# A two-layer decoder trunk: gate and up products as seven block products, and bias matmuls of 128 rows

## The chip, the cores and the metric

The kernel runs on one core of one Trainium2 chip. The metric is device time in microseconds of one launch, as the median of several runs; beside it there is one execution taken with the hardware profiler, from which all rows come. The engines are TensorE (PE; its weight loads are listed apart as PEld), VectorE (DVE), ScalarE (ACT), GpSimd (POOL) and SyncE (SP, which here only issues DMAs). A matmul takes a stationary operand of up to 128 x 128 (loaded by an LDWEIGHTS) and streams a moving operand of up to 512 columns through it, into a bank of PSUM (128 x 512 in fp32; eight banks).

## The reference

Two layers on 512 tokens of width 1024, in fp32. Each layer does, cut to what matters:

```python
z = x @ w_in + b_in                        # 11648 columns: q, k, v, gates ...
y_a = dilated window attention (3 groups of 6 heads), combined by softmax denominators
y_b = silu(g_r) * group_norm(retention(q_r, k_r, v_r))     # 4 heads
mix = (sigmoid(gate_a) * (y_a @ w_attn_proj) + sigmoid(gate_b) * (y_b @ w_ret_proj)) @ w_out
x = layer_norm(ALPHA * x + mix)
ffn = (silu(x @ w_gate) * (x @ w_up)) @ w_down             # w_gate, w_up: 1024 x 2816
x = layer_norm(ALPHA * x + ffn)
```

## The kernel before

**Precision.** Each fp32 operand is split into a high part (rounded to the matmul's format, by a ScalarE cast, L92 or L319) and a low part (the rest, by a VectorE subtraction, L93 or L325). A product a·b is three matmuls: high·high, high·low, low·high (`mm3`). x lies transposed in `xh` and `xl` (width in chunks of 128 down the partitions, tokens across), weights come by DMA into `raw` tiles (128 x 1024, eight buffers) and are split into `whi` and `wlo` (four buffers each; `unit`).

**Order.** The tile framework lays down each engine's instruction order when the kernel is built, from its own estimate of durations: among instructions it expects to be ready it takes the one that the program emits first, so a later one can move ahead into a gap. Small work (attention steps, transposes, block sums) is put between matmuls by hand: functions wait in a list `side`, and `tick`, called after every three matmuls, pops them at a set rate (`pace`). `drain` pops the rest. Each engine then runs its queue strictly in that order.

**The two ways to make a product with a weight matrix.** `wstat` makes 128 output columns for all 512 tokens: 8 chunks x 3 matmuls of 512 columns, weights stationary. `wstat_halves` does the same for four outputs in two halves of 256 tokens, for the start of a stage, where the later tokens of x aren't there yet. `tall` makes a 2 x 2 block product by the Strassen-Winograd scheme, with x stationary: seven products instead of eight, over sums S1 to S4 of blocks of x (kept in `xs`, made by `x_sums` from plain copies of x, `xc`) and sums P1 to P4 of blocks of the weights. P1 and P3 are summed by an accumulating DMA that GpSimd issues (L310), P2 and P4 by VectorE (L336). The products run in this order and add up in three PSUM chains, A, X and C:

```python
ORDER = ((1, "A11", "B11"), (2, "A12", "B21"), (5, "S1", "P1"), (3, "S4", "B22"),
         (6, "S2", "P2"), (7, "S3", "P3"), (4, "A22", "P4"))
CHAIN = {1: "A", 6: "A", 7: "A", 4: "A", 2: "X", 5: "C", 3: "C"}
```

The partial results of products 1, 5 and 6 are copied out by ScalarE (L422) before the chain goes on; after product 7 VectorE subtracts (L429). In `tall` each chain is two PSUM tiles, one for each half of the tokens (`a` in 0, 1), and the halves alternate. `tall` is used for the attention's v (288 columns a block) and for the retention's values and gates (512 a block). There, a bias is added by a matmul that opens chains A and C: `ones` (33 x 128, ones in the first and last row) times `bh` (33 rows; the first holds the high part of the bias, the last the low part, the rest zero). There are 48 of these in a launch. `bias_rows` fills them.

**The feed-forward network.** Its 2816 hidden columns are done in three parts of 3, 4 and 4 pairs of 128 (`FPARTS`); a pair needs 256 columns of gate and of up, two outputs each. The first pair goes through `wstat_halves`, the others through four `wstat`. Silu by ScalarE (L1007), the product with up by VectorE (L1012), and a split give `ht`; then the part's down projection (`xstat`) adds into the residual. The first layer norm's result reaches `xh`, `xl` by transposes (`to_xT`), four token tiles one after the other.

**The start, and the attention's tail.** At the start of layer 0, x comes in four token tiles and the first weights in four quarters; `pair_units(..., apart=True)` splits the weights quarter by quarter. In the attention, each pair of heads ends with a tail of seven steps, put between the next pair's steps at given places: `swapped` and `weighed` are DMAs on ScalarE's queue, through DRAM; `weigh` combines the groups' denominators; `scale` and `place` apply them.

Of the kernel before, what the change touches and what calls it, by code (L numbers as in the profile page):

```python
# [18 lines left out]
P = 128  # L19
# [29 lines left out]
BK = 33  # L49
# [4 lines left out]
def hybrid_kernel(ctx, tc, x, rel_bias, w_in, b_in, w_attn_proj, w_ret_proj, w_out,  # L54
# [15 lines left out]
    ones = keep.tile([BK, P], F32R, name="ones")  # L70
    bh = keep.tile([BK, 1024], F32R, name="bh")
# [124 lines left out]
    def pair_units(w, c, c2=None, apart=False):  # L196
# [9 lines left out]
        if c2 is not None:  # L206
            todo = [(hf, q) for hf in range(2) for q in range(2)]
            for hf, q in sorted(todo, key=lambda t: t[::-1]) if apart else todo:
                nc.sync.dma_start(vs[hf][:, :, q * P:(q + 1) * P], w[:, 4 * hf:4 * hf + 4, (c, c2)[q]:(c, c2)[q] + P])
        if not apart:  # L210
            return [unit(v) for v in vs]
        out_ = [tuple(view(wp.tile([P, 1024], F32R, tag=t, name=t), 4, 256) for t in ("whi", "wlo")) for _ in vs]
        for q in range(2):
            for v, (h, l) in zip(vs, out_):
                cs = slice(q * P, (q + 1) * P)
                hilo(v[:, :, cs], h[:, :, cs], l[:, :, cs])
        return out_
# [77 lines left out]
    class Right:  # L295
# [33 lines left out]
        def begin(self, n):  # L329

            if n == "B11":
                self.load("B11", "B21", "P1", "B22", "P3")
            elif n in ("P2", "P4"):
                for u in range(len(self.shapes)):
                    r = self.t["P1", u]
                    dve.tensor_tensor(out=r, in0=r, in1=self.t["B22" if n == "P2" else "B21", u], op=ALU.add)  # L336
            return self.high(n)
# [47 lines left out]

    def run(g):
        for _ in g:
            pass
# [10 lines left out]
    def bias_rows(b1, b2):  # L399

        n = b1.shape[0]
        r = raw("rb")[:BK, :2 * n]
        pool.memset(r, 0.0)
        for q in (0, BK - 1):
            pool.dma_start(r[q:q + 1, :n], b1.unsqueeze(0))
            pool.dma_start(r[q:q + 1, n:], b2.unsqueeze(0))
# [3 lines left out]
        e = slice(BK - 1, BK)  # L410
# [58 lines left out]
    def attention_pair(hp, qk, v, yp, bias, yaT):  # L469
# [107 lines left out]
        tail = [swapped, weigh, weighed, lambda: scale(0), lambda: place(0), lambda: scale(1), lambda: place(1)]  # L577
# [15 lines left out]
    def layer(ly, cp):  # L593
# [65 lines left out]
        with stage("attn") as ap_, stage("attw", 4) as aw:  # L659
# [5 lines left out]
            def qk_units(hp, g, apart=False):  # L665
                c = g * GW + hp * P
                return pair_units(w_l, C_QA + c, C_KA + c, apart)
# [9 lines left out]
            if ly == 0:  # L677
# [18 lines left out]
                us0 = [qk_units(0, 0, True)]  # L696
                load_x(2)
                us0.append(qk_units(0, 1))
                load_x(3)
# [6 lines left out]
                dve.memset(o32[:BK, :P], 0.0)  # L706
                dve.memset(o32[0:1, :P], 1.0)
                dve.memset(o32[BK - 1:BK, :P], 1.0)
                act.copy(out=ones, in_=o32[:BK, :P])
# [55 lines left out]
            for hp in range(HPG // 2):  # L765
# [10 lines left out]
                for at, f in zip((24, 22, 15, 14, 12, 8, 3), reversed(tail)):  # L776
# [5 lines left out]
            side.extend(n * 3 + tail[:1] + n * 4 + tail[1:2] + n * 3 + tail[2:5] + n * 6 + tail[5:6] + n * 2 + tail[6:])  # L782
# [211 lines left out]
        cp = []  # L994
        for part, (f0, f1) in enumerate(FPARTS):
            ht = []
            for fpair in range(f0 // 2, f1 // 2):
                ug, uu = pair_units(wg_l, fpair * 256), pair_units(wu_l, fpair * 256)
                if fpair == 0:
                    pgs = wstat_halves([(u, e) for u in (ug, uu) for e in range(2)])  # L1000
                    ln_par(ln2_g[ly], ln2_b[ly])
                else:
                    pgs = [wstat(ug, e) for e in range(2)]
                ts = []
                for e in range(2):
                    t = work("sl")
                    act.activation(out=t, in_=pgs[e], func=AF.Silu)  # L1007
                    ts.append(t)
                for e in range(2):
                    pu = pgs[2 + e] if fpair == 0 else wstat(uu, e)  # L1010
                    t = ts[e]
                    dve.tensor_tensor(out=t, in0=t, in1=pu, op=ALU.mult)  # L1012
                    o_ = fo.tile([P, 2, S], F32R, tag="op", name="ht")
                    hilo(t, o_[:, 0], o_[:, 1])
                    ht.append(o_)
                drain()

            def h_tok(k, i, ht=ht):
                return ht[k][:, 0, i * P:(i + 1) * P], ht[k][:, 1, i * P:(i + 1) * P]
# [79 lines left out]
```

## Time and profile before

| | before |
|---|---|
| runs | 2248.61 us median of 3 (2247.89 to 2251.42) |
| the profiled execution | 2250.18 us, its span 2248.4 us |
| TensorE busy | 2223.7 us, 10890 matmuls |
| weight loads busy | 1841.0 us |
| VectorE, ScalarE, GpSimd busy | 1184.3, 844.7, 180.8 us |
| DMA | 294.23 MB, 131 GB/s on average |

A row of a timeline gives start, duration, engine, line, operation and "output<-inputs", shapes, and in brackets the idle time before it with what ended it. Rows of groups give count, then total busy time and the mean of one in ns, then idle time before them by what ended it. Matmul ends are modelled, so one row's time overlaps the next; the distance between starts is what a matmul takes in a stream.

### The profile page before, as it was taken

The numbers are of one execution on the slowest core, as the hardware profiler recorded it, in microseconds if no ns is written. First come the engines' busy times: TensorE is split into PE (matmuls) and PEld (weight loads), VectorE is DVE, ScalarE is ACT, GpSimd is POOL, SyncE is SP. The second block draws the span as 40 slices with busy tenths as digits, with TensorE's granted clock in tenths as the row PEclk, the third lists the DMA queues.
The fourth block names the chain that finished last, engine by engine and source line by source line (L and its number), as shares of the span: only waits on it lengthen the run. The fifth ranks groups of instructions, "written<-read, shape, count | busy, mean of one in ns | idle before, by whom it ended". The sixth has DMA issues, their size and how long they took to land.

```text
span 2248.4 us, 27714 instructions
## 1 busy us (share of the span) xinstructions
PE 2223.7 (99%) x10890; PEld 1841.0 (82%) x10890; DVE 1184.3 (53%) x1795; ACT 844.7 (38%) x1373; POOL 180.8 (8%) x240
## 2 busy tenths in 40 slices
PE   8999999999999999999999999999999999999998
PEld 7977778878888888888889777788888888888886
DVE  5643677776245543334376446777743455333345
ACT  4444544545333132223145445445543232222230
POOL 3110011110000100000030100111000001000001
PEclk9999999999999999999999999999999999999999
DMA  7943365555655133333159343565455552333320
GB/s 213 240 128 83 74 161 151 140 133 158 216 178 187 57 113 94 94 95 111 47 155 248 98 91 86 146 167 144 125 172 195 193 169 66 101 89 101 103 76 38
DMA packets 261602, 294.23 MB, mean 131 GB/s; under 512 B 21517, under 2 KB 199841, under 8 KB 261344
## 3 DMA queue, kind: packets, MB, share of 16 engines
q1 hardware_dynamic: 212928, 234.13, 35.0%
q0 software_dynamic: 21264, 45.54, 9.1%
q10 hardware_dynamic: 27280, 12.80, 2.0%
q8 instruction: 85, 1.39, 0.3%
q14 instruction: 45, 0.37, 0.1%
HBM read 266.63 MB, written 28.53 MB: 131 GB/s over the span
## 4 chain that ended last, share of the span: by engine, by line
PE 74%; issue 16%; DMA 4%; DVE 3%; POOL 1%; ACT 1%; POOLq 0%; DVEq 0%; ACTq 0%
PE ps L81 66%; PE px L81 6%; DMA raw<-in_w_in 2%; PE px L502 1%; POOL ry L124 1%; PE px L833 1%; DMA exd<-wb 1%; DMA fa<-exd 1%; DVE wlo L325 1%; DVE xtok L926 1%; DMA rb<-in_b_in 0%; DMA exd<-pk 0%; DMA mb<-exd 0%; DVE stats L937 0%; PE px L169 0%
## 5 line engine op out<-in xcount | busy, mean ns | idle before, releaser
L81 PE MATMUL ps<-xh,whi 128*128 128x512 f32 (+1 forms) x1760 | 674.8, 385 | 7.1 <-ACT xh L92 7.1
L81 PE MATMUL ps<-xh,wlo 128*128 128x512 f32 (+1 forms) x1760 | 659.7, 375 | 1.0 <-DVE wlo L93 1.0
L81 PE MATMUL ps<-xl,whi 128*128 128x512 f32 (+1 forms) x1760 | 659.6, 375 | 0.2 <-DVE xl L93 0.2
L93 DVE TENSOR_TENSOR wlo<-raw,whi 128x1024 fp32r<-128x1024 f32 (+2 forms) x274 | 330.8, 1208 | 528.2 <-ACT whi L92 527.7
L92 ACT CAST whi<-raw 128x1024 fp32r<-128x1024 f32 (+2 forms) x274 | 282.8, 1035 | 462.9 <-PE ps L81 399.6
L81 PEld LDWEIGHTS ps<-xh,whi 128*128 128x128 f32 x1760 | 332.1, 189 | 71.3 <-ACT xh L92 8.3
L81 PEld LDWEIGHTS ps<-xh,wlo 128*128 128x128 f32 x1760 | 332.2, 189 | 61.2 <-DVE wlo L93 1.2
L81 PEld LDWEIGHTS ps<-xl,whi 128*128 128x128 f32 x1760 | 333.1, 189 | 53.7 <-DVE xl L93 1.0
L81 PE MATMUL ps<-whi,xs 128*128 128x512 f32 (+1 forms) x768 | 221.9, 363 | 0.0
L325 DVE TENSOR_TENSOR wlo<-raw,whi 128x1024 fp32r<-128x1024 f32 (+1 forms) x168 | 178.7, 1064 | 81.1 <-ACT whi L319 80.3
L319 ACT CAST whi<-raw 128x1024 fp32r<-128x1024 f32 (+1 forms) x168 | 154.2, 923 | 118.8 <-PE ps L81 92.6
L81 PE MATMUL ps<-whi,ht 128*128 128x512 f32 x576 | 178.3, 389 | 0.0
L81 PEld LDWEIGHTS ps<-whi,xs 128*128 128x128 f32 x768 | 137.7, 188 | 24.1 <-ACT whi L319 2.2
L81 PE MATMUL ps<-wlo,xs 128*128 128x512 f32 (+1 forms) x384 | 138.0, 359 | 0.4 <-DVE wlo L325 0.4
L124 POOL TENSOR_TENSOR ry<-ve,mhalf 128x1 f32<-128x1 f32 x48 | 44.8, 944 | 1152.0 <-DVE ve L123 1152.0
L81 PEld LDWEIGHTS ps<-whi,ht 128*128 128x128 f32 x576 | 108.1, 188 | 22.4
L81 PE MATMUL ps<-wlo,ht 128*128 128x512 f32 x288 | 112.0, 389 | 0.0
L81 PE MATMUL ps<-whi,xh 128*128 128x512 f32 (+1 forms) x288 | 106.7, 370 | 1.9 <-DVE sn L429 1.9
L81 PE MATMUL ps<-wlo,xh 128*128 128x512 f32 (+1 forms) x288 | 103.2, 358 | 0.0
L81 PE MATMUL ps<-whi,xl 128*128 128x512 f32 (+1 forms) x288 | 103.0, 358 | 0.0
L310 POOL DMA_DIRECT2D raw<-in_w_in x48 | 59.2, 1234 | 293.0 <-DMA raw<-in_w_in 204.0
L81 PEld LDWEIGHTS ps<-wlo,xs 128*128 128x128 f32 x384 | 72.2, 188 | 9.6 <-DVE wlo L325 0.9
(167 smaller groups left out, 2518.9 us busy)
## 6 DMA issues: line engine op xcount, KB each, us to landing
raw<-in_w_in SPq DMA_DIRECT2D x144, 512.0 KB, 4.0
raw<-in_w_ffn_gate SPq DMA_DIRECT2D x44, 512.0 KB, 3.8
raw<-in_w_ffn_up SPq DMA_DIRECT2D x44, 512.0 KB, 3.8
raw<-in_w_ffn_down SPq DMA_DIRECT2D x44, 512.0 KB, 3.7
raw<-in_w_in SPq DMA_DIRECT2D x72, 256.0 KB, 5.3
raw<-in_w_in POOLq DMA_DIRECT2D x32, 512.0 KB, 7.4
raw<-in_w_ret_proj SPq DMA_DIRECT2D x32, 512.0 KB, 3.9
raw<-in_w_in SPq DMA_DIRECT2D x40, 288.0 KB, 4.3
```

What stands on the lines that cost most here:

```text
L81: pe.matmul(ps, lhsT=a, rhs=b, start=start, stop=stop, skip_group_check=True)
L92: act.copy(out=hi, in_=src)
L93: dve.tensor_tensor(out=lo, in0=src, in1=hi.bitcast(F32), op=ALU.subtract)
L124: pool.tensor_tensor(out=y, in0=ve, in1=mhalf, op=ALU.pow)
L310: pool.dma_start(r, self.src({"P1": "B12", "P3": "B22"}[n], u), accum_op=ALU.add)
L319: act.copy(out=h, in_=src)
L325: dve.tensor_tensor(out=l, in0=src, in1=h.bitcast(F32), op=ALU.subtract)
L502: pe.transpose(px[:, (2 + j) * P:(3 + j) * P], s[:, hh, j * P:(j + 1) * P], ident)
L833: pe.transpose(px[:, t * P:(t + 1) * P], ys[i][:, t * P:(t + 1) * P], ident)
L926: dve.scalar_tensor_tensor(out=o_, in0=o_, scalar=rs, in1=b_[:, c:c + n], op0=ALU.mult, op1=ALU.add)
```

## The change

Every gate/up pair but a layer's first becomes one seven-product block product (`wide`, `ffn_pair`), with the weights stationary and x's blocks moving: the "1" columns are up and the "2" columns gate, 256 each; the token halves are x's blocks. A chain is one PSUM tile, with the two 128-column halves (`q`) side by side. The x copies `xc` and block sums are now also made after the first layer norm. The bias matmuls get 128 rows, with the low part in row 32 as before. P3 is loaded ahead of B22. At the start of layer 0 two token tiles are transposed before the first weights are split, the bias columns' buffers come from the work pool, and the attention's tail steps move in the list.

```diff
-BK = 33
+BK = 32
-    ones = keep.tile([BK, P], F32R, name="ones")
-    bh = keep.tile([BK, 1024], F32R, name="bh")
+    ones = keep.tile([P, P], F32R, name="ones")
+    bh = keep.tile([P, 1024], F32R, name="bh")
...
-                self.load("B11", "B21", "P1", "B22", "P3")
+                self.load("B11", "B21", "P1", "P3", "B22")
...
+    def wide(right, left, ev):
+
+        ps = {}
+        for (i, an, bn), ((h, l),) in zip(ORDER, right.operands()):
+            c = CHAIN[i]
+            if i in FIRST:
+                ps[c] = psum("ps")
+            for q in range(2):
+                cs = slice(q * P, (q + 1) * P)
+                for k in range(4):
+                    ah, al = left(an, k, slice(0, 256))
+                    mm3(ps[c][:, q * 256:(q + 1) * 256], h[:, k, cs], l[:, k, cs], ah, al,
+                        i in FIRST and q == 0 and k == 0, k == 3)
+                    tick(STEP / 2)
+            if i != 3:
+                ev(i, ps[c])
+            if i == 6:
+                ev(3, ps["C"])
+            yield
...
-        tail = [swapped, weigh, weighed, lambda: scale(0), lambda: place(0), lambda: scale(1), lambda: place(1)]
+        tail = [swapped, weigh, lambda: scale(0), lambda: place(0), weighed, lambda: scale(1), lambda: place(1)]
...
-        braws.append(sm.tile([COLS // P, P], F32, tag="braw", name="braw", bufs=2))
+        braws.append(work("braw")[:COLS // P, :P])
...
-                for f in ops[0]:
+                for f in ops[0] + ops[1]:
                     f()
-                side.extend(ops[1] + [lambda l_=l_: bias_cols(l_) for l_ in range(DEPTH)] + vecs[:3] + ops[2] + vecs[3:] + ops[3])
+                make()
+                us0 = [first, qk_units(0, 1)]
+                load_x(3)
+                side.extend([lambda l_=l_: bias_cols(l_) for l_ in range(DEPTH)] + vecs[:3] + ops[2] + vecs[3:] + ops[3])
...
-                for at, f in zip((24, 22, 15, 14, 12, 8, 3), reversed(tail)):
+                for at, f in zip((26, 24, 18, 16, 14, 12, 3), reversed(tail)):
...
+            xc = [[mp.tile([P, 4, 256], F32, name=f"xc{a}{b}") for b in range(2)] for a in range(2)]
...
-                        side.extend([nothing] * (6, 2, 4, 5)[i] + to_xT(xt[:, i], i, None))
+                        side.extend([nothing] * (6, 2, 4, 5)[i] + to_xT(xt[:, i], i, xc))
...
-        fo = fin.enter_context(stage("fo", 11))
+        fo = fin.enter_context(stage("fo", 5))
...
+        def ffn_plain(f, o_):
+
+            ug, uu = pair_units(wg_l, f * P), pair_units(wu_l, f * P)
+            pgs = wstat_halves([(u, e) for u in (ug, uu) for e in range(2)])
+            drain()
+            side.extend(x_sums(xc))
+            pace(8)
...
+        def ffn_pair(f, o_):
+
+            def src(b, u):
+                k = 4 if b[1] == "2" else 0
+                return (wg_l if b[2] == "2" else wu_l)[:, k:k + 4, f * P:f * P + 256]
...
+            def ev(i, ps):
+                p2 = ps.rearrange("p (q t) -> p q t", q=2)
+                if i in (1, 5, 6):
+                    sn[i] = work("sn").rearrange("p (q t) -> p q t", q=2)
+                    act.copy(out=sn[i], in_=p2)
+                elif i == 2:
+                    dve.tensor_tensor(out=sn[1], in0=p2, in1=sn[1], op=ALU.add)
+                elif i == 3:
+                    v = sn[6]
+                    dve.tensor_tensor(out=v, in0=p2, in1=v, op=ALU.subtract)
+                    act.activation(out=v, in_=v, func=AF.Silu)
+                    dve.tensor_tensor(out=v, in0=v, in1=sn[1], op=ALU.mult)
+                    put(v, slice(0, 256))
+                elif i == 7:
+                    dve.tensor_tensor(out=sn[5], in0=sn[5], in1=p2, op=ALU.subtract)
+                    act.activation(out=sn[5], in_=sn[5], func=AF.Silu)
+                elif i == 4:
+                    v = sn[5]
+                    dve.tensor_tensor(out=v, in0=v, in1=p2, op=ALU.mult)
+                    put(v, slice(256, 512))
+
+            run(wide(Right(src, [(4, 256)]), x_left, ev))
```

The attention's last tail, after the third pair of heads, is spread over 32 places instead of 25 in the same 42 us.

More of the change, by code (lines that the diff above doesn't have):

```diff
@@ L401, in bias_rows @@
         n = b1.shape[0]
-        r = raw("rb")[:BK, :2 * n]
+        r = raw("rb")[:, :2 * n]
         pool.memset(r, 0.0)
-        for q in (0, BK - 1):
+        for q in (0, BK):
             pool.dma_start(r[q:q + 1, :n], b1.unsqueeze(0))
@@ L994, in layer @@
         cp = []
+        def ffn_plain(f, o_):
[4 more added lines that the diff above has]
+            pace(8)
+            for e in range(2):
+                t = work("sl")
+                act.activation(out=t, in_=pgs[e], func=AF.Silu)
+                dve.tensor_tensor(out=t, in0=t, in1=pgs[2 + e], op=ALU.mult)
+                hilo(t, o_[:, 0, e], o_[:, 1, e])
@@ L995, in layer @@
         for part, (f0, f1) in enumerate(FPARTS):
             ht = []
[L997 to L1000, printed above, removed]
-                    ln_par(ln2_g[ly], ln2_b[ly])
[L1002 to L1016, printed above, removed]
+            for f in range(f0, f1, 2):
+                ht.append(fo.tile([P, 2, 2, S], F32R, tag="op", name="ht"))
+                (ffn_pair if f else ffn_plain)(f, ht[-1])
+                if f == 2:
+                    drain()
+                    ln_par(ln2_g[ly], ln2_b[ly])
```

49 lines of the change are left out of this document (26 added, 23 removed).

## The prediction

> **What bounds the kernel now.** I read the engine totals first, then the stages, then single matmuls.
>
> ```profile
> span 2248.4 us, 27714 instructions
> PE 2223.7 (99%) x10890; PEld 1841.0 (82%) x10890; DVE 1184.3 (53%) x1795; ACT 844.7 (38%) x1373; POOL 180.8 (8%) x240
> 330.00:560.00 230.00, 230.00 (x1036) 186.87 (x1035) 168.17 (x254) 114.26 (x154) 24.40 (x33) 1.00 0.52 140
> 802.00:867.00 65.00, 65.00 (x288) 53.81 (x288) 24.00 (x25) 16.64 (x20) 0.00 (x0) 1.00 0.33 98
> ```
>
> The first two lines are the page's. The other two are a table by stage: length, then busy time of TensorE, weight loads, VectorE, ScalarE and GpSimd, granted clock, DMA share and GB/s. TensorE is the bound: 99% busy, with a clock of 1.00 and no idle time in the retention values and gates (330 to 560) or in three gate/up pairs (802 to 867). But "busy" doesn't say how fast matmuls follow one another, so the reader should look at starts.
>
> ```profile
> 829.24 0.39 PE L81 MATMUL ps<-xl,whi 128*128 128x512 f32 x1
> 829.46 0.39 PE L81 MATMUL ps<-xh,wlo 128*128 128x512 f32 x1
> 829.69 0.39 PE L81 MATMUL ps<-xh,whi 128*128 128x512 f32 x1
> 1151.00 0.28 PE L81 MATMUL ps<-xl,whi 128*128 128x256 f32 x1
> 1151.12 0.28 PE L81 MATMUL ps<-xh,wlo 128*128 128x256 f32 x1
> 343.58 0.39 PE L81 MATMUL ps<-whi,xs 128*128 128x512 f32 x1
> 343.90 0.50 PE L81 MATMUL ps<-bh,ones 33*128 33x512 f32 x1
> 344.32 0.50 PE L81 MATMUL ps<-whi,xs 128*128 128x512 f32 x1
> 344.66 0.39 PE L81 MATMUL ps<-wlo,xs 128*128 128x512 f32 x1
> 343.89 0.18 PEld L81 LDWEIGHTS ps<-bh,ones 33*128 33x128 f32 x1 [0.35 <-issue]
> 344.32 0.19 PEld L81 LDWEIGHTS ps<-whi,xs 128*128 128x128 f32 x1 [0.24 <-issue]
> ```
>
> In the timeline of TensorE a 512-column matmul starts about 0.227 us after the last (829.24 to 829.69 is 0.45 for two), a 256-column one 0.120. Around a bias matmul, three starts take 344.66 - 343.58 = 1.08 instead of 3 x 0.227 = 0.68: 0.40 us lost, because its weights are loaded only as it starts, and those of the next only when it is through.
>
> **The change, part by part.** The sum is made against the profiled execution, 2250.2 us (span 2248.4); the median of the runs, 2248.6, is 0.07% below it, so I take the same difference off it.
>
> *Seven products.* A gate/up pair is now 4 outputs x 8 chunks x 3 = 96 matmuls of 512 columns: 96 x 0.227 = 21.79 us. `wide` makes 7 products x 2 column halves x 4 chunks x 3 = 168 of 256 columns: 168 x 0.120 = 20.16. The saving is not the eighth that arithmetic promises (2.72), since 256 columns cost more than half of 512. Ten pairs in each of two layers: 20 x 1.63 = **-32.6 us**.
>
> *Hand-overs inside a pair.* `wide` keeps each sum in one PSUM tile. Product 3 adds to C right behind product 5, 7 to A behind 6, and 4 to A behind 7; between them ScalarE must copy the tile (twice) or VectorE subtract it (once). `tall` does two token halves, so the other half covered this. Nothing in the old gate/up stage shows it; the nearest rows:
>
> ```profile
> 830.82 0.39 PE L81 MATMUL ps<-xh,wlo 128*128 128x512 f32 x1
> 831.25 0.69 DVE L1012 TENSOR_TENSOR sl<-sl,ps 128x512 f32<-128x512 f32 x1 [3.32 <-PE ps L81]
> L422 ACT COPY sn<-ps 128x512 f32<-128x512 f32 x48 | 28.1, 586 | 21.5 <-PE ps L81 21.3
> 289.24 0.40 PE L81 MATMUL ps<-whi,xs 128*128 128x512 f32 x1
> 289.56 0.67 DVE L429 TENSOR_TENSOR sn<-sn,ps 128x512 f32<-128x512 f32 x1
> 290.38 0.47 PE L81 MATMUL ps<-whi,xh 128*128 128x512 f32 x1 [0.74 <-DVE sn L429]
> 14.51 0.58 PE L81 MATMUL ps<-xh,whi 128*128 128x256 f32 x1 [6.07 <-ACT xh L92]
> 14.89 0.35 PE L590 MATMUL px<-ident,braw 91*128 91x91 f32 x1
> ```
>
> VectorE starts 0.43 us after the last matmul's start (830.82 to 831.25); for 256 columns 0.32, as those take 0.28 and not 0.39. TensorE goes on 0.15 after VectorE is done (289.56 + 0.67 to 290.38). So a bare hand-over costs 0.32 + 0.59 + 0.15 - 0.12 = 0.94 by ScalarE and 1.04 by VectorE: 2.9 us a pair, **+58** in all. At 289.24 such a wait did cost 1.14 - 0.23 = 0.91. The other end is 0: at 14.89 a transpose of the bias columns, which the program emits 24 matmuls later, runs behind the first matmul, so the build's ordering fills a gap that it foresees. Here product 6 (input ready, other tile) can fill the first hand-over, and the next pair's product 1 the others: its cast needs the buffer that product 3 freed 2.9 us earlier. A gain is excluded. I take the end that the last rows speak for, with one 0.12 us slot left at each: 60 x 0.12 = **+7**.
>
> *VectorE and ScalarE in a pair.*
>
> ```profile
> L325 DVE TENSOR_TENSOR wlo<-raw,whi 128x1024 fp32r<-128x1024 f32 x112 | 136.4, 1219 | 51.1 <-ACT whi L319 51.1
> L336 DVE TENSOR_TENSOR raw<-raw 128x1024 f32<-128x1024 f32 x32 | 39.0, 1220 | 0.8
> L319 ACT CAST whi<-raw 128x1024 fp32r<-128x1024 f32 x112 | 116.8, 1048 | 74.8 <-PE ps L81 63.1 <-DMA y_d<-yt 10.5 <-ACT yb L828 1.0
> ```
>
> VectorE: 7 low parts x 1.22 + 2 sums for P2 and P4 x 1.22 + 7 half-size steps x 0.69 = 15.8 us of 20.2, 78%. ScalarE: 7 x 1.05 + 3 copies, 2 Silus and 2 casts at about 0.6 = 11.5. Both lie beside TensorE; in 330 to 560 VectorE was 168/230 = 73% busy with TensorE never idle. **0**; if the cover goes, it shows in the hand-overs.
>
> *Loads.* A pair brings 7 pieces of 0.52 MB instead of 4: 3.67 MB in 20.2 us, 182 GB/s, two of them added by GpSimd's queue. A pair takes five of the eight buffers, so most of the next pair's loads can be issued a pair ahead. P3 before B22 lets the second accumulation start a load earlier. The stage that had 193 GB/s:
>
> ```profile
> 560.00:680.00 120.00, 120.00 (x535) 99.34 (x534) 42.87 (x45) 39.00 (x45) 4.05 (x6) 1.00 0.58 193
> ```
>
> TensorE never waited there: **0**.
>
> *Bias matmuls of 128 rows.* Their number stays 48. Is it the 33 rows?
>
> ```profile
> L81 PE MATMUL ps<-bh,ones x48: 393/498/502, 56.0 to 1603.1; 33*128 33x512 f32 x32, 33*128 33x288 f32 x16
> L81 PE MATMUL px<-qk 64*128 64x256 f32 x72 | 12.6, 428 | 0.0
> L81 PE MATMUL px<-rot 128*128 128x256 f32 x48 | 7.0, 282 | 0.0
> L407 DVE TENSOR_TENSOR rb<-rb 33x512 f32<-33x512 f32 x8 | 5.4, 681 | 4.7 <-DMA rb<-in_b_in 4.7
> ```
>
> With the same 256 columns, 64 rows are recorded at 428 ns and 128 rows at 282, so rows short of 128 do cost. At 128 rows the loss should go entirely; taking the 0.40 for the 16 of 288 columns too, 48 x 0.40 = **-19.2** (bounds 0 and -19.2). Filling and adding 128 rows instead of 33 costs 0: 33 x 512 takes VectorE 681 ns, 128 x 512 the 0.69 us of the row at 831.25, and it lies beside TensorE.
>
> On this the Trainium skill ("TensorE: Matmul & The Clock Gate", Part 2 and the table under "Why this matters for your kernels") speaks against the change: it gives a matmul of 32 rows the time of one of 128, and a weight load's time as independent of rows. By that alone this term would be 0 and the sum 2222 us; the trace's 428 against 282 ns speak against it.
>
> *Start.* Both token tiles' transposes and casts now come ahead of the first weights' casts.
>
> ```profile
> PE ps L81 <- ACT xh L92: 7.1, 5, 6.1
> 8.68 0.62 ACT L92 CAST whi<-raw 128x512 fp32r<-128x512 f32 x1 [1.34 <-DMA raw<-in_w_in]
> 13.35 0.62 ACT L92 CAST whi<-raw 128x512 fp32r<-128x512 f32 x1 [0.43 <-DMA raw<-in_w_in]
> 13.88 1.06 ACT L92 CAST xh<-px 128x512 fp32r<-128x512 f32 x2
> ```
>
> TensorE waited 6.1 us for the casts of x, of which the last three (0.53 each) stood in ScalarE's queue among or behind four weight casts, 8.68 to 13.35, that each awaited their DMA. With x first, the first weight cast moves from 8.68 to about 10.3, and the first matmul from 14.5 to near there: **-4** (0 to -6).
>
> *What layer 0 gives back.*
>
> ```profile
> 80.00:90.00 10.00, 9.67 (x62) 8.31 (x61) 3.79 (x6) 4.25 (x9) 3.56 (x3) 1.00 1.01 230
> 75.17 13.29 DMA raw<-in_w_in x2
> ```
>
> From 40 to 110 the DMA engines are full, and at 88.46 TensorE just meets a load that took 13.29. Start and eight bias matmuls (3.2) reach it 7 us early; I let half be lost: **+4** (0 to +7).
>
> *Attention's weights.* The swap's reader moves from place 8 to 12 in the list.
>
> ```profile
> 203.73 0.17 DVE L536 TENSOR_TENSOR mn<-nm,mb 128x8 f32<-128x8 f32 x1 [4.04 <-DMA mb<-exd]
> 206.21 1.43 PE L81 MATMUL px<-v,sT 128*128 128x64 f32 x8 [3.04 <-ACT sT L503]
> 207.97 0.63 PE L81 MATMUL ps<-xl,whi 128*128 128x512 f32 x1
> ```
>
> Late by a DMA, it held ScalarE, and TensorE idled 3.04 us and then ran seven matmuls recorded like the last row, 0.63 instead of 0.39 (1.7 us). Four places are some 4 us, but the build may pull the step forward again: **-3** (0 to -6).
>
> *Entry to the feed-forward network.* Eight copies of 0.6 us on ScalarE and four block sums with high and low parts (VectorE 8 x 1.22 = 9.8 us) are new in each layer; they lie beside the second half of the first pair and two products. S1, wanted third, has the least slack: +1 a layer, **+2** (0 to +6). Eleven single buffers become five double ones; only finished products need them: 0.
>
> Sum: -32.6 + 7 - 19.2 - 4 + 4 - 3 + 2 = -45.8. 2250.2 - 45.8 = 2204.4 profiled; 2248.6 - 45.8 = **2203 us** for the runs.
>
> **The rivals.**
> - *Hand-overs partly filled*, 0.25 to 0.7 us each: 60 x that instead of 7 gives 2211 to 2238. For it: the build foresees durations, and at 289.24 it didn't. 14%.
> - *Slower: hand-overs bare.* The gain without this term is 52.8 us, so from 52.8/60 = 0.88 us each the kernel is no faster. At 58 it is 2254, and more if an eviction stands behind a 1.22 us low part in a queue 78% full. For it: 0.91 at 289.24; against: the filled gap at 14.89. 9%, some of it inside the noise.
> - *The bias matmuls don't do it*: rows aren't the cause, but the switch to other operands. Then -19.2 is 0: 2222. For it: the bias matmul also changes operands; against: the 428 against 282 ns and the two late loads. The Trainium skill's rule above leads to the same time. 7%.
> - *All small terms at their good ends*: -5 each at the start and the attention, nothing given back, no hand-over or entry cost: 2187. 4%.
> - *Forecast*: 66%, 2190 to 2216.
>
> **Range and chances.** 2188 to 2234 holds the forecast, the bias rival and most of the first. No change can be told from 0.2%, 4.5 us. Faster by more: 66 + 14 + 7 + 4 = 91%; within it 4%; slower 5%.
>
> **What would show it.** In the new profile: 12,330 matmuls on TensorE; gate/up pairs of 20.2 us after the first pair of a layer; bias matmuls of 128 rows that start like their neighbours; no wait of TensorE on the evictions in `ffn_pair`; the first weight matmul near 10; no 3 us gap near 206. Wrong I would be if waits of TensorE on the ScalarE copies and VectorE subtractions of `ffn_pair` sum to tens of us, if the bias matmuls keep their gaps, or if VectorE's low parts arrive late with a DMA behind them.

## The result, and the profile after

| | before | after |
|---|---|---|
| runs | 2250.02 us (median of 4) | 2225.74 us (median of 4, 2222.78 to 2228.9) |
| the profiled execution | 2250.18 us, span 2248.4 | 2224.68 us, span 2222.9 |
| ratio | | 0.9893, 95% interval 0.9875 to 0.9911 |

The kernel became 24 us faster. The time lies in the predicted range, and the sign is as predicted, but the forecast was 2203: the gain is about half of the 45.8 us that were summed up. That the time still lies in the range is owed to the range's width, and not to the sum. So most of this part is about the missing half.

The page of the profile after, first its span and engine totals:

```profile
span 2222.9 us, 31189 instructions
PE 2184.1 (98%) x12330; PEld 1884.7 (85%) x12330; DVE 1352.1 (61%) x1971; ACT 946.8 (43%) x1517; POOL 233.5 (11%) x280
```

The 12,330 matmuls are there. TensorE's busy time fell by 39.6 us (2223.7 to 2184.1) and the span by 25.5: work went, and part of it came back as waiting. What TensorE waits for in the whole execution, as engine, line, waited for; total, times, longest:

```profile
PE ps L81 <- DVE wlo L329: 11.6, 16, 1.4
PE ps L81 <- ACT whi L92: 3.3, 1, 3.3
...
```

The first row was 0.4 us, one wait, in the kernel before: TensorE now waits for low parts of weights (L329 is before's L325). The same view, cut to the first layer's feed-forward network (757 to 1115 us), has the same cause:

```profile
PE ps L81 <- DVE wlo L329: 4.5, 6, 0.8
PE ps L81 <- ACT whi L323: 0.8, 1, 0.8
```

That is seven waits a layer, one at each boundary between two block-product pairs that follow each other directly (1, 3 and 3 in the three parts). None of these rows names an eviction of `ffn_pair` (L1050 to L1064), of which the prediction was afraid. Only the weight loads wait for evictions, and shortly; the same view for PEld has

```profile
PEld ps L81 <- ACT sn L1050: 1.7, 9, 0.2
```

The chain of waits from 870 to 900 us shows the pattern twice; columns are start, duration and what the chain ran through:

```profile
...
873.63 1.24 DVE wlo L329
...
890.90 3.15 issue
894.05 1.05 ACT whi L323
...
895.13 1.24 DVE wlo L329
...
896.41 3.60 PE ps L81 x28
```

Read it from one boundary to the next: the low part starts at 873.63 and again at 895.13, so a pair takes 21.50 us, not 20.16. It ends in a cast, a low part, and TensorE, one behind the other. The timeline there:

```profile
894.05 1.05 ACT L323 CAST whi<-raw 128x1024 fp32r<-128x1024 f32 x1 [3.15 <-issue]
895.13 2.54 DVE L329 TENSOR_TENSOR wlo<-raw,whi 128x1024 fp32r<-128x1024 f32 x2 [3.46 <-ACT whi L323]
895.24 0.29 PE L81 MATMUL ps<-xh,whi 128*128 128x256 f32 x1
895.37 0.28 PE L81 MATMUL ps<-xl,whi 128*128 128x256 f32 x1
896.41 0.39 PE L81 MATMUL ps<-xh,wlo 128*128 128x256 f32 x1 [0.75 <-DVE wlo L329]
```

The three matmuls are the next pair's first product. The build placed them right there, as a filler for the hand-over after product 6: the order on TensorE is 13 of P2's matmuls (as filler for the hand-over before B22's), B22's 24, the other 11 of P2's, then these. The cast ahead of them waits for one of the four `whi` buffers, and the eighth weight unit in a row takes the one that B22 frees. Behind B22 there are only 11 x 0.12 = 1.3 us of TensorE's work, while cast and low part need 1.05 + 1.23 = 2.3. From 895.37 to 896.41 is 1.04, where a 256-column matmul takes 0.12: 0.92 lost.

Against before, stage by stage from the starts of matmuls (each layer's first gate/up matmul, the first values of the attention, and so on; two layers, us):

```
                                            predicted   measured
start to first scores' values, layer 0         -3.2       -1.8
attention, values and gates, layer 0           -9.4       -7.2
v stage, layer 1                               -3.2       -1.3
attention, values and gates, layer 1           -6.4       -6.5
feed-forward network, both layers             -23.6       -9.3
sum                                           -45.8      -26.1
```

From the last down matmul to the end the kernel is 0.6 us longer, so the span fell by 25.5. Of the 19.7 us that are missing, 14.3 are in the feed-forward network. Three feed-forward questions follow (the buffer, the hand-overs, what a pair costs without either), then the bias matmuls and the small terms.

### The profile page after: what moved, and what is told of

Its sections match the earlier page's. It is cut to its first block, busy times and chain, and to the rows that moved or that the text cites. A ratio compares the mean times of both kernels' runs of the same rounds, so it can differ in the third digit from the quotient of the medians.

```text
span 2222.9 us, 31189 instructions
## 1 busy us (share of the span) xinstructions
PE 2184.1 (98%) x12330; PEld 1884.7 (85%) x12330; DVE 1352.1 (61%) x1971; ACT 946.8 (43%) x1517; POOL 233.5 (11%) x280
## 3 DMA queue, kind: packets, MB, share of 16 engines
q8 instruction: 96, 1.57, 0.3%
## 4 chain that ended last, share of the span: by engine, by line
PE 80%; issue 10%; DMA 5%; DVE 3%; ACT 2%; POOL 1%; SPq 0%; POOLq 0%; DVEq 0%; ACTq 0%
PE ps L81 72%; PE px L81 6%; DMA raw<-in_w_in 3%; DVE wlo L329 1%; ACT whi L323 1%; PE px L526 1%; PE px L858 1%; DVE wlo L93 0%; POOL ry L124 0%; DMA rb<-in_b_in 0%; PE px L169 0%; DMA exd<-pk 0%; DVE xtok L951 0%; DMA exd<-wb 0%; ACT whi L92 0%
## 5 line engine op out<-in xcount | busy, mean ns | idle before, releaser
L81 PE MATMUL ps<-xh,whi 128*128 128x512 f32 (+1 forms) x1600 | 562.6, 353 | 5.9 <-ACT whi L92 3.3
L81 PE MATMUL ps<-xh,wlo 128*128 128x512 f32 (+1 forms) x1600 | 546.5, 342 | 10.5 <-DVE wlo L329 9.0
L81 PE MATMUL ps<-xl,whi 128*128 128x512 f32 (+1 forms) x1600 | 544.9, 341 | 0.2 <-DVE xl L93 0.2
L329 DVE TENSOR_TENSOR wlo<-raw,whi 128x1024 fp32r<-128x1024 f32 (+1 forms) x308 | 349.4, 1136 | 183.4 <-ACT whi L323 180.3
L323 ACT CAST whi<-raw 128x1024 fp32r<-128x1024 f32 (+1 forms) x308 | 300.4, 979 | 303.1 <-PE ps L81 176.9
L93 DVE TENSOR_TENSOR wlo<-raw,whi 128x1024 fp32r<-128x1024 f32 (+2 forms) x194 | 232.4, 1200 | 300.1 <-ACT whi L92 299.4
L81 PE MATMUL ps<-xs,whi 128*128 128x256 f32 (+1 forms) x1536 | 315.1, 302 | 0.0
L81 PEld LDWEIGHTS ps<-xs,whi 128*128 128x128 f32 x1536 | 248.7, 191 | 13.8 <-ACT sn L1050 3.5
L81 PE MATMUL ps<-xs,wlo 128*128 128x256 f32 (+1 forms) x768 | 229.9, 301 | 0.0
L81 PEld LDWEIGHTS ps<-xs,wlo 128*128 128x128 f32 x768 | 146.5, 191 | 5.4 <-DVE wlo L329 0.4
```

The source lines that it names most:

```text
L81: pe.matmul(ps, lhsT=a, rhs=b, start=start, stop=stop, skip_group_check=True)
L93: dve.tensor_tensor(out=lo, in0=src, in1=hi.bitcast(F32), op=ALU.subtract)
L323: act.copy(out=h, in_=src)
L329: dve.tensor_tensor(out=l, in0=src, in1=h.bitcast(F32), op=ALU.subtract)
```

## The experiments

All ratios are to the kernel before, on the same chip; its medians were 2250.5 to 2251.6 us.

**Two PSUM tiles a chain** (two_psum_tiles). The kernel after, with each chain in two tiles, one for each column half:

```diff
-            if i in FIRST:
-                ps[c] = psum("ps")
             for q in range(2):
+                if i in FIRST:
+                    ps[c, q] = psum("ps")[:, :256]
...
-            if i != 3:
-                ev(i, ps[c])
+                if i != 3:
+                    ev(i, q, ps[c, q])
...
```

The evictions in `ev` are halved in the same way.

> The changed kernel, but each chain of a block-product pair is two PSUM tiles, one per 128-column half, evicted half by half, as the older block product does. Theory (the loss is the hand-over, bare or badly filled): the other half's twelve matmuls, 1.44 us, cover an eviction of about 1 us; hardly any fillers are needed, the 0.9 us waits and the 0.1 to 0.2 us ones go, 14 to 18 us less than the changed kernel, 38 to 42 us below before. Rival (VectorE and ScalarE fill up: nine more evictions a pair, each half-size one costing more than half, and VectorE at some 85%): waits of TensorE on low parts of other units, 20 to 30 us below before.

2206.59 us, ratio 0.9796 (0.9783 to 0.981): about 20 us less than after, and a few more than expected. TensorE's waits in the first layer's feed-forward network (757 to 1115 us):

```profile
PE ps L81 <- DVE wlo L93: 1.0, 1, 1.0
PE ps L81 <- ACT xh L92: 0.2, 1, 0.2
```

Neither belongs to a block-product pair. The wait of 1.0 us comes at 1109.80, behind the last down matmul (1107.46), where layer 1 begins, and the kernel before has it too (0.97 at 1133.77); it has the 0.2 as well. Now an eviction in a pair, with the work beside it:

```profile
889.53 0.37 ACT L1049 COPY sn<-ps 128x256 f32<-128x256 f32 x1 [0.47 <-PE ps L81]
889.57 0.28 PE L81 MATMUL ps<-xs,wlo 128*128 128x256 f32 x1
```

While ScalarE copies one half (0.37 us), TensorE runs the other: nothing has to be found to fill the gap, so almost nothing of the next pair is moved ahead and no cast meets an occupied buffer. A pair takes 20.42 us. That is 1.34 us less than before's 21.76, or 26.8 over the 20 pairs; seven products and hand-overs together were forecast at 25.6. The scheme is thus worth what was predicted; after loses it at the pair's seams. (The Trainium skill, "Perfetto Trace Analysis", section "Matmuls" under "Optimizing Tensor Performance", says to rotate independent groups through PSUM banks so that an eviction overlaps the next group's matmuls. Here one chain's two halves do it, and the runs agree, by some 20 us.)

**One more buffer, in three places** (one_more_buffer, own_buffer_early, own_buffer_apart). Two tiles take away hand-over and filler at once. To tell buffer from hand-over, the kernel after keeps one tile a chain, and each pair's first product gets a `whi` and `wlo` of its own:

```diff
+                p_ = self.first if n == "B11" else wp
-                h = view(wp.tile([P, 1024], F32R, tag="whi", name="whi"), a, b)
+                h = view(p_.tile([P, 1024], F32R, tag="whi", name="whi"), a, b)
...                                        # the same for wlo
         fo = fin.enter_context(stage("fo", 5))
+        fw = fin.enter_context(stage("fw"))
...
-            run(wide(Right(src, [(4, 256)]), x_left, ev))
+            run(wide(Right(src, [(4, 256)], fw), x_left, ev))
```

> The changed kernel, but the first unit of each block-product pair (B11) has a whi/wlo buffer pair of its own, so five instead of four. Theory (the matmuls of the next pair that fill the hand-over from product 6 to 7 wait for their low part, whose buffer product 3 gives up too late): the fourteen waits of 0.9 us at the pairs' ends go, 12 to 13 us less than the changed kernel, which puts it 36 to 38 us below before. Rival (VectorE, 78% busy, is late by its queue, not by the buffer): the waits stay, 24 us below before. Second rival (raw buffers and loads): the waits move to ScalarE casts behind a DMA, 24 to 30 us below.

2237.38 us (0.9936, 0.9924 to 0.9949): slower than after, where 12 to 13 us less were expected. The seven waits are gone from the trace, but one of 8 us a layer has come at the first pair. To see whether it came from the buffer's place, the next kernel (own_buffer_early) sets it aside ahead of `fo`:

> The kernel after, with a high/low buffer of its own for each pair's first product, as in one_more_buffer, but set aside ahead of the buffers of ht, so that it lies where the finished m was and not where the copies of x still are. Theory: the 0.9 us waits of TensorE, seven a layer, come from the next pair's first product taking the buffer that B22 frees; the 8 us wait of one_more_buffer came from the place of the buffer alone. Then both are gone: about 353 us instead of 359.6 from a layer's first gate/up matmul to its last down matmul, 2212 us in all (2207 to 2217). Rival 1: what runs ahead waits for something else next (VectorE's queue, a raw buffer), and the small waits stay: 2220 to 2226. Rival 2: the place had nothing to do with it, and the 8 us wait stays: 2237.

2234.78 us (0.9927, 0.9913 to 0.9941). My theory of the place fell as I had put it: the 8 us wait stays. The timeline of own_buffer_early there:

```profile
783.77 0.28 PE L81 MATMUL ps<-xh,wlo 128*128 128x256 f32 x1
...
788.58 1.22 DVE L93 TENSOR_TENSOR xs<-xc,xs 128x1024 fp32r<-128x1024 f32 x1
...
790.74 1.04 ACT L324 CAST whi<-raw 128x1024 fp32r<-128x1024 f32 x1
...
791.84 0.58 PE L81 MATMUL ps<-xh,whi 128*128 128x256 f32 x1 [7.79 <-ACT whi L324]
```

TensorE stands from 783.77 until the first product's cast (790.74) is done, and that comes only after the last reader of `xc` (788.58 + 1.22 = 789.80), wherever the buffer lies. The wait also costs more than its own length: the granted clock is 0.50 from 791 to 796, where matmuls of 256 columns start 0.21 us apart instead of 0.12, and the first layer's feed-forward network takes 365.0 us, 10.7 more than in the third kernel, which has no such wait. So one buffer more made the kernel slower.

`xc` and m share one pool, so it looked as if the whole pool were the unit. In the third kernel `xc` moves into a pool on the other side of the memory, and the extra buffer shares its place with m alone (shown against one_more_buffer; own_buffer_early already had `fw` ahead of `fo`):

```diff
-        with stage("mp") as mp:
+        with stage("xcp", side="right") as xcp, stage("mp") as mp:
...
-            xc = [[mp.tile([P, 4, 256], F32, name=f"xc{a}{b}") for b in range(2)] for a in range(2)]
+            xc = [[xcp.tile([P, 4, 256], F32, name=f"xc{a}{b}") for b in range(2)] for a in range(2)]
...
+        fw = fin.enter_context(stage("fw"))
         fo = fin.enter_context(stage("fo", 5))
-        fw = fin.enter_context(stage("fw"))
```

> As own_buffer_early, but the copies of x lie in a pool of their own on the other side of the memory, so that the extra buffer shares its place with the finished m alone. Theory: in own_buffer_early and one_more_buffer the extra buffer came free only with the last sum over the copies of x, because both were in one pool; so the build put the first pair's first cast behind those sums on ScalarE, and TensorE met it 8 us late. Apart, that wait is gone too, and so are the seven 0.9 us waits a layer: 2219.5 us (2217 to 2222), 355.5 us from a layer's first gate/up matmul to its last down matmul. What is left against two_psum_tiles (350) are then gaps of 0.1 to 0.3 us at the hand-overs. Rival: the build puts that cast late for another reason, and the 8 us wait stays: 2234.

2214.0 us (0.984, 0.9826 to 0.9853), 3 us better than the expected range, the 8 us wait gone and with it the seven small ones. Its timeline has the first pair's cast before the pair is due:

```profile
758.46 1.05 ACT L324 CAST whi<-raw 128x1024 fp32r<-128x1024 f32 x1
```

and its waits of TensorE from 757 to 1115 us hold only one row, for weights of another kind (L93; 0.96 of it at 1114.61, again where layer 1 begins):

```profile
PE ps L81 <- DVE wlo L93: 1.2, 2, 1.0
```

So the buffer is shown as the cause of the 0.92 us waits: in all three kernels that have it they are gone. What moving `xc` alone would do was not tried. What remains of the hand-overs is small. The waits of the weight loads (PEld) in the same stretch of own_buffer_apart:

```profile
PEld ps L81 <- ACT sn L1052: 3.3, 17, 0.2
...
PEld ps L81 <- DVE sn L1062: 0.6, 2, 0.3
```

and one such gap in its timeline:

```profile
908.44 1.05 ACT L324 CAST whi<-raw 128x1024 fp32r<-128x1024 f32 x1 [1.83 <-PE ps L81]
909.39 0.58 ACT L1052 COPY sn<-ps 128x512 f32<-128x512 f32 x1
909.75 0.77 PE L81 MATMUL ps<-xs,whi 128*128 128x256 f32 x3
910.36 0.28 PE L81 MATMUL ps<-xs,wlo 128*128 128x256 f32 x1
```

Three matmuls take 0.61 from start to start instead of 0.36: a hand-over by ScalarE costs 0.25 us here, with fillers. The copy stands behind a cast in ScalarE's queue and ends at 909.97, a little after the 13 fillers that the build gave it. Together, from the starts of matmuls (a pair is 168 of 256 columns):

```
                    one pair    first gate/up to last down matmul, layer 0 / 1
predicted            20.16 + 0.36 at hand-overs     352.4 / 351.0
two_psum_tiles       20.42                          350.6 / 349.2
own_buffer_apart     20.71                          354.3 / 352.7
after                21.50                          359.6 / 358.2
before               21.76                          364.2 / 362.8
```

From after to own_buffer_apart is 10.8 us over both layers: the buffer. That is 0.77 for each of the 14 waits; the rest of what each one lost is a hand-over's 0.25, which own_buffer_apart pays at the same place. From there to two_psum_tiles is 7.2: the hand-overs.

**Where two tiles and the extra buffer meet** (two_tiles_p1_early_own_buffer) is told below, as it has the load order too.

**The bias matmuls alone** (bias_rows_only): the kernel before, with 128 rows in `ones` and `bh`, the low part in row 32.

```diff
-BK = 33
+BK = 32
-    ones = keep.tile([BK, P], F32R, name="ones")
-    bh = keep.tile([BK, 1024], F32R, name="bh")
+    ones = keep.tile([P, P], F32R, name="ones")
+    bh = keep.tile([P, 1024], F32R, name="bh")
...
```

> The kernel before, with the bias matmuls of 128 rows and nothing else. Theory (rows short of 128 keep weight loads from running ahead): each of the 48 loses its 0.40 us of gaps, so 16 to 19 us less than before, up to 3 of the 19 being given back in layer 0's v stage, where the loads were just in time. Rival (it is the switch of operands, not the rows): the starts around a bias matmul stay 0.3 to 0.4 us apart and the time is that of before, within 2 us.

2238.76 us (0.9942, 0.9929 to 0.9956): 13 us, less than I expected. Yet at the bias matmuls nothing is left to gain:

```profile
343.67 0.39 PE L81 MATMUL ps<-whi,xs 128*128 128x512 f32 x1
343.90 0.39 PE L81 MATMUL ps<-bh,ones 128*128 128x512 f32 x1
344.13 0.39 PE L81 MATMUL ps<-whi,xs 128*128 128x512 f32 x1
```

Starts are 0.23 apart, as in any stream. Over all 48, the time above the plain distance was 19.1 us before and is 1.1 here: 18.0 gone, as forecast. But the trace as a whole is 10.9 us shorter. The rest came back as waits, most of them in the v stage. The rows there:

```profile
72.14 0.46 DVE L407 TENSOR_TENSOR rb<-rb 128x288 f32<-128x288 f32 x1 [4.06 <-DMA rb<-in_b_in]
...
72.64 0.67 ACT L409 CAST bh<-rb 128x576 fp32r<-128x576 f32 x1 [3.65 <-DVE rb L407]
...
73.79 0.39 ACT L422 COPY sn<-ps 128x288 f32<-128x288 f32 x1
...
74.23 0.40 PE L81 MATMUL ps<-whi,xs 128*128 128x288 f32 x1 [1.96 <-ACT sn L422]
...
1197.60 0.40 PE L81 MATMUL ps<-whi,xs 128*128 128x288 f32 x1 [0.68 <-ACT whi L319]
```

A bias row's DMA lands late, VectorE waits 4.06 us for it, ScalarE stands behind in `bh`, and the copy that TensorE needs stands behind that: 1.96 us at 74.23. In layer 1 it is a late cast of weights (1197.60). The first of these waits is that execution's own: in bias_96_rows below, which is as fast, the bias row lands in time, and the waits of the same stage, 2.3 us, end in weight casts and low parts. So that the stage gives back is shown, and what holds it in the end is not. In layer 0 the v stage gave back more than it had gained, in layer 1 half; the values and gates kept 5.3 and 5.6 of 6.4 us a layer.

**How many rows** (bias_96_rows): the same with 96 rows.

> As bias_rows_only, but 96 rows instead of 128. Theory 1: any number of rows short of 128 keeps the next weight load from being pulled ahead: the bias matmuls lose 0.40 us each as with 33 rows, time as before, 2250 us. Theory 2: the loss goes with the number of rows or ends at some number below 96: gaps as with 128 rows, 2239 us; or in between.

2239.24 us (0.9948, 0.993 to 0.9966), as with 128:

```profile
341.18 0.39 PE L81 MATMUL ps<-whi,xs 128*128 128x512 f32 x1
341.41 0.40 PE L81 MATMUL ps<-bh,ones 96*128 96x512 f32 x1
341.64 0.40 PE L81 MATMUL ps<-whi,xs 128*128 128x512 f32 x1
```

So "rows short of 128 do cost", as I had put it, is too wide: 96 cost nothing, 33 cost 0.40 us. The rival that the switch of operands is the cause is out, as the operands still switch here. The trace of the kernel before narrows the limit down, as it has matmuls of 64 rows (the attention's scores) between those of 128:

```profile
109.64 0.39 PE L81 MATMUL ps<-xh,wlo 128*128 128x512 f32 x1
109.96 0.49 PE L81 MATMUL px<-qk 64*128 64x128 f32 x4
110.39 0.50 PE L81 MATMUL ps<-xh,whi 128*128 128x512 f32 x1
110.72 0.39 PE L81 MATMUL ps<-xl,whi 128*128 128x512 f32 x1
```

The first of them starts 0.32 after its 512-column neighbour instead of 0.23, and the first matmul of 128 rows behind them holds the next one off for 0.33. Around a bias matmul of 33 rows these distances were 0.32 and 0.34. So 64 rows cost as 33 do at both ends, though these matmuls start in pairs, 0.007 apart, and are no exact counterpart; a limit in the number of rows would lie between 64 and 96. The Trainium skill ("TensorE: Matmul & The Clock Gate", section "LDWEIGHTS (loading the stationary operand)") says that a load of 32 rows takes as long as one of 128. The record of a load agrees (183 ns for 33 rows, 188 for 128); what differs is when the loads start, so a matmul of few rows costs more in a stream than the load's time tells.

**The load order** (b22_before_p3): after with the old order of P3 and B22.

> The changed kernel with the old load order, B22 ahead of P3. Theory (loading P3 first makes B22, wanted two products earlier, late in the attention's v stage): the waits at the fourth product there (1.7 us near 1187, and some 2 of layer 0's near 87) go, 2 to 4 us less than the changed kernel, 26 to 28 us below before. Rival (the accumulating load of P3 is then the late one): waits at the sixth product instead, 20 to 24 us below before.

2224.9 us (0.9879, 0.9865 to 0.9892): no difference that can be told, and the waits near 1187 stay. My theory that P3's earlier load makes them falls.

**P1 ahead of B21** (two_tiles_p1_early, after_p1_early). First on two_psum_tiles, then on after itself:

```diff
-                self.load("B11", "B21", "P1", "P3", "B22")
+                self.load("B11", "P1", "B21", "P3", "B22")
```

> As two_psum_tiles, with the loads of P1's two parts issued ahead of B21's. Theory: the waits of the v stage (2.3 us at 83 to 87 in layer 0, 1.8 at 1175 to 1178 in layer 1) end with a cast whose input is P1's accumulating load, so an earlier load takes them away: 2202.5 us (2200 to 2205). Rival: the eight raw buffers set the time of the load, not its place in the order, or B21 is late in its stead: no change or slower, 2206 to 2210.

2198.33 us (0.9763, 0.975 to 0.9777): faster by more than expected, and not where I expected it, so the gain was luck: the v stage's waits are still there in its trace (2.5 us near 84 to 89, 2.1 at 1173); the gain lies between the attention's first values and the feed-forward network.

> The kernel after (one PSUM tile a chain) with the loads of P1's two parts issued ahead of B21's. Of two_tiles_p1_early's gain of 8 us the trace shows none in the v stage and nearly all in the attention, where the tail's reader no longer waits 3.8 us for its DMA. Theory: the other load order makes the build place the tail's DMA earlier, whatever the feed-forward network does: about the same gain here, 2218 us (2215 to 2221). Rival: it fell well in that one kernel only: 2223 to 2227 here, with the waits of the attention as in after.

2216.28 us (0.9844, 0.983 to 0.9857), 9 us less than after, so it isn't special to two tiles. The place was only half foreseen: by the starts of matmuls 4.1 us come from before the attention's first values in layer 0 and 0.5 from the v stage of layer 1, the other 4.1 from the attention and the values and gates. In the attention the DMA that the tail's reader needs is issued earlier; in after

```profile
197.64 0.38 ACTq L554 DMA_DIRECT2D mb<-exd  x1
...
200.91 0.17 DVE L560 TENSOR_TENSOR mn<-nm,mb 128x8 f32<-128x8 f32 x1 [3.93 <-DMA mb<-exd]
```

and in after_p1_early

```profile
190.78 0.38 ACTq L554 DMA_DIRECT2D mb<-exd  x1
...
192.95 0.17 DVE L560 TENSOR_TENSOR mn<-nm,mb 128x8 f32<-128x8 f32 x1
```

VectorE no longer waits 3.93 us for it, and TensorE's waits behind it in the attention (4.1 us in after, in both layers together) are gone. Why the build issues it earlier when weights of another stage load in another order is not shown.

**The tail and the start** (old_tail, old_start). After, with one of the two put back:

```diff
-        tail = [swapped, weigh, lambda: scale(0), lambda: place(0), weighed, lambda: scale(1), lambda: place(1)]
+        tail = [swapped, weigh, weighed, lambda: scale(0), lambda: place(0), lambda: scale(1), lambda: place(1)]
...
-                for at, f in zip((26, 24, 18, 16, 14, 12, 3), reversed(tail)):
+                for at, f in zip((24, 22, 15, 14, 12, 8, 3), reversed(tail)):
...                                        # the last tail over 25 places again
```

> The kernel after, with the attention tail's steps in the old order and at the old places. Theory: of the 26 us that the trace of after is shorter, about 3.3 come from the tail's move. Then TensorE's gap of some 3 us near 200 is back, and the time is 2229 us (2227 to 2231). Rival: the gap went because the steps around it fell differently, not because of the list: no difference, 2224 to 2226.5.

2223.63 us (0.988, 0.9867 to 0.9894): no difference to after, though the single long wait is back:

```profile
205.71 1.47 PE L81 MATMUL px<-v,sT 128*128 128x64 f32 x8 [2.56 <-ACT sT L527]
```

In after there were two short ones in its place (0.7 us at 201 and 1.6 at 210), and two like them in layer 1 (0.56 and 1.57), where old_tail has one of 0.94. With a wait of 0.6 in old_tail's layer 0, the attention's waits sum to 4.1 us in both kernels. So the tail's move is worth about nothing.

```diff
                 first, make = qk_units(0, 0, pair_apart)
+                make()
...
-                for f in ops[0] + ops[1]:
+                for f in ops[0]:
                     f()
-                make()
...
-                side.extend([lambda l_=l_: bias_cols(l_) for l_ in range(DEPTH)] + vecs[:3] + ops[2] + vecs[3:] + ops[3])
+                side.extend(ops[1] + [lambda l_=l_: bias_cols(l_) for l_ in range(DEPTH)] + vecs[:3] + ops[2] + vecs[3:] + ops[3])
```

> The kernel after, with layer 0's first weights split ahead of the transposes of x and the second token tile's transposes back among the small work. Theory: the first weight matmul moves from 12.4 back to about 14.5 us, and what the start saved is kept further on: 2227.5 us (2226.5 to 2229), the first scores 2 to 3 us later than in after. Rival (the prediction's): layer 0's v stage, which waits for its loads, gives back half or more: 2225 to 2226.5, and the first scores at most 1 us later.

2225.78 us (0.989, 0.9877 to 0.9904): no difference. The first weight matmul in the timeline of after

```profile
12.38 0.39 PE L81 MATMUL ps<-xh,whi 128*128 128x256 f32 x1 [3.30 <-ACT whi L92]
```

and of old_start

```profile
14.33 0.58 PE L81 MATMUL ps<-xh,whi 128*128 128x256 f32 x1 [6.00 <-ACT xh L92]
```

and the row of the attention's values (count, shortest/median/longest in ns, first start to last), whose first follows the first scores, in after

```profile
L81 PE MATMUL px<-v,sT x360: 217/275/323, 116.2 to 1346.4; 128*128 128x64 f32 x180
```

and in old_start

```profile
L81 PE MATMUL px<-v,sT x360: 217/275/323, 116.3 to 1345.0; 128*128 128x64 f32 x180
```

1.95 us earlier at 12, 0.1 us earlier at 116: the start's gain is given back whole, where the prediction's step on layer 0 let half be lost. (Single traces scatter here: in the nine other kernels with after's start the first weight matmul comes at 10.9 to 12.2. The medians of the runs say the same.)

**All that helped together** (two_tiles_p1_early_own_buffer): two tiles, P1 early, and the buffer apart.

> two_tiles_p1_early with the extra buffer of own_buffer_apart. Theory: with two PSUM tiles a chain the build hardly moves anything ahead between the products, so no cast waits for a buffer, and the extra one changes nothing: 2198 us (2196 to 2200). Rival: the first pair's first product can also start earlier in a layer: 1 to 3 us less.

2195.45 us (0.9753, 0.974 to 0.9767): the fastest kernel here. Its interval overlaps that of two_tiles_p1_early, so the extra buffer's part, some 3 us, is not shown; a pair takes 20.42 us as without it, and the feed-forward networks of both layers together differ by 0.2 us.

## Why the prediction was right or wrong

- *Seven products, -32.6:* right. With the seams covered a pair takes 20.42 us against 20.16 worked out from 168 x 0.120 (and 21.76 before, against 21.79).
- *Hand-overs inside a pair, +7:* the step that failed; with the buffer it came to some 23 us (32.6 less the 9.3 that the feed-forward network gained). Its price for a filled hand-over was nearly right: own_buffer_apart pays 0.55 us a pair above 20.16, where I took 0.36. What failed is the sentence that the next pair's first product can fill the later ones, since "its cast needs the buffer that product 3 freed 2.9 us earlier". The buffer is the right one, but fillers shift the order: when the cast can start, TensorE has 1.3 us of work left before the filler, and cast and low part take 2.3. Seven times a layer that costs 0.92 us, 12.8 us in all, and a buffer more takes 10.8 of it away. I had checked that the buffer comes free before the filler's place in the program, not the place that the build would give it. This is the rival "partly filled" in size (23/60 is 0.38 us each), with a mechanism that no rival named. The time lies nearest to the rival "the bias matmuls don't do it" (2222), but by chance: their gaps are gone. Bare hand-overs at 0.9 us each didn't come.
- *VectorE and ScalarE in a pair, 0* and *Loads, 0:* right. TensorE waited for no load in the feed-forward network, and VectorE's lateness there was that of its input.
- *Bias matmuls of 128 rows, -19.2:* right at the matmuls (18.0 of 19.1 us gone), wrong for the kernel: alone it gave 10.9 us in the trace and 13 in the runs. Most of the loss is the v stage's, which in layer 1, too, waits for weights and small work as soon as TensorE is faster; I had allowed for that in layer 0 only. The reason I gave (any row short of 128) was too wide: 96 rows cost nothing.
- *Start, -4:* half right. The gain is 2.1 us in this trace (14.5 to 12.4, not 10.3): TensorE waits 3.3 us for the first cast of weights, which now stands behind those of x. *What layer 0 gives back, +4:* right in kind and about in size: start and v stage together came to -1.8 instead of -3.2.
- *Attention's weights, -3:* wrong. The wait of 3 us became two of 2.3 together, layer 1 got 2.1 where it had 0.6, and old_tail is no slower than after.
- *Entry to the feed-forward network, +2:* not seen. In two_psum_tiles TensorE has only the wait of 0.24 us there that before has too.

In sum, of the 19.7 us missing, 10.8 are the buffer, some 4 the hand-overs (0.55 instead of 0.36 us a pair, 20 pairs), and the other 5 gains of the bias matmuls and the small terms that were given back. The first two are shown by runs; the last is a difference, and only its size is.

## What to carry to other kernels

When a stage relies on other work to fill its gaps, follow the filler's own inputs: count the buffers between it and what it displaces, and compare the work left on the engine with the cast and the low part that must run after the buffer comes free. Better, make the gap coverable by construction: two PSUM tiles a chain cost nothing and were worth 20 us. And a gain at single matmuls counts only in stages that TensorE bounds; in a stage that waits for loads or small work, price the wait that stands behind it.

## What was not expected of the hardware

- A stationary operand of 96 rows costs a stream nothing (341.18, 341.41, 341.64), one of 33 rows 0.40 us, and those of 64 rows show the same distances at their two ends (0.32 and 0.33).
- A wait of TensorE of 7.79 us cost 10.7: behind it the granted clock was 0.50 for some 5 us. The waits of 0.75 left it at 1.00.
- A hand-over inside a PSUM tile cost 0.25 us here even with other matmuls in between (0.61 for three matmuls of 0.12), as the copy stood behind a cast, and half-size evictions of 0.37 us under the other half left 0.26 us a pair in all.
- The same gap of 0.92 us repeating 14 times was a buffer that was missing. (The Trainium skill, "Perfetto Trace Analysis", section "Optimization Strategy", says that consistent bubbles on the engine that should be saturated can mean too little memory for the next tile to be allocated; here an own buffer took them away, worth 10.8 us.)
